# The second FFN projection of a decoder block in seven block products over all 22 k tiles

## The chip, the core and the metric

One Trainium2 chip, one of its cores. The kernel is one launch on that core; the metric is the device time of one execution in microseconds. The program's work is spread over the core's engines, which run side by side and each take their own instructions in order: TensorE (PE; its weight loads are listed apart as PEld), VectorE (DVE), ScalarE (ACT), GpSimd (POOL) and SyncE (SP). SP issues most of the DMAs, POOL and ACT some.

## The reference

One decoder block for 512 tokens of width 1024, in float32: a conditioned RMSNorm, one wide input projection, a gated MLP mixer beside sparse attention, an output projection with a gated residual, and then the FFN. What matters here is the end of it:

```python
x = x + gate1 * (merged @ w_out)
h2 = rms_norm(x, norm2_g) * (1.0 + scale2) + shift2
f_g, f_u = jnp.split(h2 @ w_ffn_in, 2, axis=-1)        # 1024 -> 2 x 2816
x = x + gate2 * ((jax.nn.silu(f_g) * f_u) @ w_ffn_out) # 2816 -> 1024
return rms_norm(x, final_norm_g)
```

The second FFN projection multiplies the gated activations, 512 tokens by 2816, with `w_ffn_out`, 2816 by 1024. 2816 is 22 k tiles of 128.

## The kernel before

**Precision.** TensorE multiplies rounded float32 (fp32r). Every operand is therefore split in a high part (ACT copies it to fp32r) and a low part (DVE subtracts the high part from the source), and a product is three matmuls: high by high, high by low, low by high (`mm3`, lines 53 to 55).

**The stream of weights.** `stream` is a list, in order of use, of weight chunks of 512 KB (128 partitions by two k tiles by 512 columns in the last stage). `issue` starts a chunk's DMA on SP into one of three `raw` buffers, `prep` makes its high part on ACT (line 112) and its low part on DVE (line 116) into one of three `hi` and three `lo` buffers, and `get(i)` prepares up to the second chunk after `i`. So ACT's copy for a chunk waits until TensorE has left the chunk three places before it.

**Seven products in place of eight.** Three projections are computed as 2 by 2 block matrices with seven block products and sums of blocks (Winograd's form): the output projection in part (`oprod`), the first FFN projection (the loop over `q` from line 1627), and the second FFN projection (`zprod`, line 1736). In the second FFN projection, a block is 256 tokens by ten k tiles and ten k tiles by 512 columns: 20 of the 22 k tiles (`KZ`). The two other k tiles (`KC`, 20 and 21) are multiplied in the ordinary way, between the fifth and the sixth product: `W_FO`, lines 1807 to 1813, 48 matmuls of 512 columns. The products come in the order A11, S1, S2, A12, S3, A22, S4. Each is five chunks; for each chunk there are two token tiles of 128, with six matmuls each. Results lie in the eight PSUM banks, and are copied or added between banks where a product contributes to several output blocks (`z_copy`, `z_out`, `z_add`).

**The activations' blocks and their sums.** `a_hi`, `a_lo` and `a_sum` make the high part, the low part and the difference for part `c` of a block, three parts to a block (four, four and two k tiles). They are listed by hand as tasks beside the chunks of each `zprod`: a chunk's tasks are issued after `get` for that chunk and ahead of its matmuls.

**The weights' sums.** The sums of weight blocks are made in DRAM by DMAs that POOL issues, and that copy or accumulate (`wsum_steps`, lines 292 to 314): five groups, one for each chunk position, of six steps; steps 0 and 1 have two DMAs each, the others one. Step 1 accumulates onto what step 0 wrote, step 2 copies what step 1 made, step 3 accumulates onto that, and so on. One call of `wstep` (line 318) issues the next step: ACT writes one element (line 323), POOL copies it (line 324, which ties POOL to ACT's place in the program), and POOL issues the DMAs (lines 305 and 307). After every three steps one call is empty. The loop over `q` has 20 rounds with two calls each, and these 40 calls use up the list of 30 steps and 10 empty places.

**The output projection.** Lines 1418 to 1470 finish it: for each half of the tokens and each half of the columns, two chunks of weights, so eight blocks of twelve matmuls. Between them DVE adds the residual (`resid`), ACT makes the sums of squares, and `row_rstd` (line 1237) gives each token tile its scale: DVE reduces, and POOL raises to the power -1/2 (line 1239). `row_rstd` for tiles 0 and 1 comes after the fourth block, for tiles 2 and 3 after the eighth. `norm2_x` scales the tokens with it (on DVE for even tiles, line 1253, on ACT for odd ones, line 1251), and `norm2_T` transposes them on TensorE (line 1273) and hands them to ACT (lines 1278 and 1281) and DVE (line 1282). Tiles 0 and 1 are transposed within the last block, tiles 2 and 3 within the first groups of the FFN, which otherwise follow at once (line 1599).

**The end.** During A22 and S4, `res_` adds the residual of an output tile that is final (lines 1229 and 1230 on DVE, 1231 on ACT) and multiplies it with the final gain (line 1715 on DVE). `done` finishes a token tile. The last chunks of S4 run token tile by token tile: tile 0 in matmuls of 512 columns, tile 1 in matmuls of 256.

Of the kernel before, what the change touches and what calls it, by code (L numbers as in the profile page):

```python
# [28 lines left out]
def block_kernel(ctx: ExitStack, tc: tile.TileContext, x, positions, w_ada, b_ada, w_in,  # L29
# [239 lines left out]
    KZ = ([0, 1, 2, 3, 4, 5, 6, 7, 12, 13], [8, 9, 10, 11, 16, 17, 18, 19, 14, 15])  # L269
    KC = [20, 21]  # L270
    NZ = 5

    dram = ctx.enter_context(tc.tile_pool(name="dram", bufs=1, space=bass.MemoryType.DRAM))
    wsum = {n: dram.tile([NZ * 256, 512], F32, name=f"wsum{n}") for n in (1, 2, 3, 4)}
    W_Z = {}

    def add_z(key):
        W_Z[key] = []
        for c in range(NZ):
            if key in wsum:  # L280
                src, k0, c0 = wsum[key], 2 * c, 0
            else:
                src, k0, c0 = w_ffn_out, KZ[key[0]][2 * c], key[1] * 512
            W_Z[key].append(add_w(src, [k0, k0 + 1], c0, 512))

    for key in ((0, 0), 1, 2, (1, 0), 3):
        add_z(key)
    W_FO = [add_w(w_ffn_out, KC, 512 * h, 512) for h in range(2)]
    for key in (4, (1, 1)):
        add_z(key)  # L290

    def wsum_steps():

        def step(c, *moves):
            o = slice(256 * c, 256 * c + 256)

            def fn():
                for n, add, src in moves:
                    if isinstance(src, tuple):
                        k = KZ[src[0]][2 * c] * 128  # L300
                        src = w_ffn_out[k:k + 256, 512 * src[1]:512 * src[1] + 512]
# [16 lines left out]
    def wstep():  # L318

        fn = wsteps.pop(0) if wsteps else None  # L320
        if fn:
            t = sm[:, 20 + len(wsteps):21 + len(wsteps)]
# [1095 lines left out]
    for half in range(2):  # L1418
        for h in range(2):
# [124 lines left out]
    za = {}  # L1544
# [7 lines left out]
    def a_part(name, c):  # L1552
        kh, th = AT_[name]
        t = gz[((0, 1, 3), (2, 4, 3))[kh][c]]
        if c == 2:
            t = t[:, 2 * kh:2 * kh + 2]
        return t[:, :, th * 256:(th + 1) * 256]

    def a_hi(key, c):
        h = ZA[key][c]  # L1560
        if c == 2:
# [164 lines left out]
    def zmm(o, ka, c, e, w, cc, start, stop):  # L1726
        ah, al = za[ka, c // 2]
        wh, wl = w
        for j in range(2):
            k_ = 2 * (c % 2) + j  # L1730
            a = tuple(t[:, k_, e * 128:(e + 1) * 128] for t in (ah, al))
            mm3(o, a, (wh[:, j, cc], wl[:, j, cc]), start and j == 0, stop and j == 1, skip_group_check=True)
# [41 lines left out]
    fng, gs = [], []  # L1774
# [5 lines left out]
    def g_hi():  # L1780
        t = ffn[0].tile([128, 2, 2, S], F32R, name="gs", tag="E0", bufs=1)
        gs.extend((t[:, 0], t[:, 1]))
        A.activation(gs[0], gz[5], AF.Copy)

    def g_lo():
        V.tensor_sub(gs[1], gz[5], f(gs[0]))

    zprod(0, "A11", (0, 0), True, [[outs_left, hi_("S1", 0)], [lo_("S1", 0), hi_("S1", 1)],
                                   [lo_("S1", 1), hi_("S1", 2), sm_("S2", 1), lo_("S1", 2)],
                                   [sm_("S2", 2), hi_("S2", 0)], [lo_("S2", 0), hi_("S2", 1)]])  # L1790
    z_copy(1, 0, -1.0)
    zprod(3, "S1", 1, True, [[lo_("S2", 1), hi_("S2", 2), sm_("S4", 0), lo_("S2", 2)], [sm_("S4", 1), hi_("A12", 0)],
                             [sm_("S4", 2), lo_("A12", 0)], [hi_("A12", 1)],
                             [lo_("A12", 1), hi_("A12", 2)]])
    z_out(3)
    zprod(1, "S2", 2, False, [[lo_("A12", 2), sm_("S3", 0)], [sm_("S3", 1)], [sm_("S3", 2), hi_("S3", 0)],
                              [lo_("S3", 0), hi_("S3", 1)], [lo_("S3", 1), hi_("S3", 2)]])
    z_copy(2, 1, -1.0)
    zprod(0, "A12", (1, 0), False, [[lo_("S3", 2), hi_("A22", 0)], [lo_("A22", 0), lambda: z_add(1, 3, V.tensor_add)],
                                    [hi_("A22", 1)], [lo_("A22", 1), hi_("A22", 2)], [lo_("A22", 2)]])  # L1800
    zprod(2, "S3", 3, False, [[hi_("S4", 0)], [lo_("S4", 0), hi_("S4", 1)], [lo_("S4", 1), hi_("S4", 2)],
# [109 lines left out]
```

## Time and profile before

| | |
|---|---|
| median of three runs | 824.95 us (824.74 to 825.56) |
| the profiled execution | 825.28 us |
| its span, first to last instruction | 823.4 us |
| TensorE busy | 808.5 us, 98% of the span |
| VectorE busy | 684.9 us, 83% |
| ScalarE, GpSimd busy | 427.7 us and 156.5 us |
| output projection's last eight blocks | from about 455.6 us |
| first FFN projection | from 479.7 us |
| second FFN projection | from 705.9 us, last matmul at 815.7 us |

The views of the profile used below are the page's summary, the busy times by stretches of time, the waits of an engine, and the timeline of an engine. A timeline's row gives start and length in microseconds, the engine, the source line, the operation, what it writes and reads, and in brackets how long the engine stood idle before it and what ended that. A matmul's length is modelled; since matmuls overlap, what one costs is the distance between the starts.

### The profile page before, as it was taken

The numbers are of one execution on the slowest core, as the hardware profiler recorded it, in microseconds if no ns is written. First come the engines' busy times: TensorE is split into PE (matmuls) and PEld (weight loads), VectorE is DVE, ScalarE is ACT, GpSimd is POOL, SyncE is SP. The second block draws the span as 40 slices with busy tenths as digits, with TensorE's granted clock in tenths as the row PEclk, the third lists the DMA queues.
The fourth block names the chain that finished last, engine by engine and source line by source line (L and its number), as shares of the span: only waits on it lengthen the run. The fifth ranks groups of instructions, "written<-read, shape, count | busy, mean of one in ns | idle before, by whom it ended". The sixth has DMA issues, their size and how long they took to land.

```text
span 823.4 us, 12920 instructions
## 1 busy us (share of the span) xinstructions
PE 808.5 (98%) x4920; PEld 722.0 (88%) x4920; DVE 684.9 (83%) x1167; ACT 427.7 (52%) x760; POOL 156.5 (19%) x171
## 2 busy tenths in 40 slices
PE   7999999999999999999999999999999999999996
PEld 6889889988888888988888899999999999888785
DVE  7989788798899558887688879889989888798676
ACT  6674444323332226665636586555555556666543
POOL 3060031362354411000000010222212222000001
PEclk9999999999999999999999999999999999999998
DMA  9974352332346553046630504889988978766543
GB/s 293 311 211 119 103 179 78 107 100 91 112 136 199 185 174 102 26 153 209 198 132 12 194 27 138 200 263 244 288 221 237 213 220 185 226 203 205 180 128 128
DMA packets 107197, 138.46 MB, mean 168 GB/s; under 512 B 6480, under 2 KB 77136, under 8 KB 106976
## 3 DMA queue, kind: packets, MB, share of 16 engines
q1 hardware_dynamic: 96832, 109.76, 42.8%
q0 software_dynamic: 9584, 27.07, 14.1%
q8 instruction: 38, 0.62, 0.3%
q10 hardware_dynamic: 720, 0.82, 0.3%
q14 instruction: 23, 0.19, 0.1%
HBM read 135.26 MB, written 23.07 MB: 192 GB/s over the span
## 4 chain that ended last, share of the span: by engine, by line
PE 51%; DVE 19%; DMA 5%; ACT 2%; issue 2%; POOL 0%; POOLq 0%; ACTq 0%; DVEq 0%
PE R L53 6%; PE R L54 6%; PE R L55 6%; DMA mraw<-in_w_ada_dram 5%; PE pfo L55 3%; PE pfo L54 3%; PE pfo L53 3%; DVE acc L177 3%; DVE sco L717 2%; DVE m L713 2%; PE pb L53 2%; PE pb L55 2%; PE pb L54 2%; DVE lo L116 2%; PE po L54 2%
## 5 line engine op out<-in xcount | busy, mean ns | idle before, releaser
L112 ACT ACTIVATE hi<-raw 128x1024 fp32r<-128x1024 f32 (+2 forms) x103 | 107.0, 1040 | 106.0 <-PE pb L54 35.7
L116 DVE TENSOR_TENSOR lo<-raw,hi 128x1024 fp32r<-128x1024 f32 (+2 forms) x67 | 81.1, 1214 | 29.4 <-ACT hi L112 28.9
L116 POOL TENSOR_TENSOR lo<-raw,hi 128x1024 fp32r<-128x1024 f32 x29 | 73.0, 2521 | 128.1 <-ACT hi L112 122.4
L53 PE MATMUL pb<-h,hi 128*128 128x512 f32 (+1 forms) x192 | 74.6, 388 | 0.0
L55 PE MATMUL pb<-h,lo 128*128 128x512 f32 (+1 forms) x192 | 73.9, 385 | 0.0
L54 PE MATMUL pb<-h,hi 128*128 128x512 f32 (+1 forms) x192 | 73.9, 385 | 0.0
L54 PE MATMUL pfo<-lo,za 128*128 128x512 f32 (+1 forms) x146 | 56.4, 386 | 0.3 <-DVE lo L116 0.3
L55 PE MATMUL pfo<-hi,za 128*128 128x512 f32 (+1 forms) x146 | 56.2, 385 | 0.0
L53 PE MATMUL pfo<-hi,za 128*128 128x512 f32 (+1 forms) x146 | 56.2, 385 | 0.0
L177 DVE SCALAR_TENSOR_TENSOR acc<-mraw,cols,acc 128x512 f32<-128x512 f32 x49 | 39.8, 813 | 19.6 <-DMA mraw<-in_w_ada_dram 18.6
L1239 POOL TENSOR_TENSOR sm<-sm,mhalf 128x1 f32<-128x1 f32 x8 | 5.3, 660 | 216.9 <-DVE sm L1238 216.9
L53 PE MATMUL R<-tb,sx 128*128 128x256 f32 x160 | 45.3, 283 | 1.1 <-ACT R L1661 0.7
L54 PE MATMUL R<-tb,sx 128*128 128x256 f32 x160 | 45.1, 282 | 0.0
L55 PE MATMUL R<-tb,sx 128*128 128x256 f32 x160 | 45.0, 281 | 0.0
L55 PE MATMUL R<-tb,lo 128*128 128x256 f32 x160 | 44.8, 280 | 0.0
L53 PE MATMUL R<-tb,hi 128*128 128x256 f32 x160 | 44.8, 280 | 0.0
L54 PE MATMUL R<-tb,hi 128*128 128x256 f32 x160 | 44.6, 279 | 0.0
L55 PEld LDWEIGHTS pb<-h,lo 128*128 128x128 f32 x192 | 36.0, 188 | 7.3
L54 PEld LDWEIGHTS pb<-h,hi 128*128 128x128 f32 x192 | 36.0, 188 | 6.9
L53 PEld LDWEIGHTS pb<-h,hi 128*128 128x128 f32 x192 | 36.0, 188 | 6.9
L324 POOL COPY sm<-sm 128x1 f32<-128x1 f32 x30 | 18.9, 631 | 117.0 <-ACT sm L323 116.9
L54 PE MATMUL pav<-lo,h 128*128 128x256 f32 x128 | 35.8, 279 | 0.0
(377 smaller groups left out, 2675.4 us busy)
## 6 DMA issues: line engine op xcount, KB each, us to landing
raw<-in_w_ffn_in_dram SPq DMA_DIRECT2D x44, 512.0 KB, 5.8
raw<-in_w_in_dram SPq DMA_DIRECT2D x40, 512.0 KB, 3.8
wsum<-in_w_ffn_out_dram POOLq DMA_DIRECT2D x30, 512.0 KB, 7.0
mraw<-in_w_ada_dram SPq DMA_DIRECT2D x28, 512.0 KB, 4.1
raw<-wsum SPq DMA_DIRECT2D x20, 512.0 KB, 3.9
raw<-in_w_ffn_out_dram SPq DMA_DIRECT2D x18, 512.0 KB, 4.5
s<-in_w_ada_dram SPq DMA_DIRECT2D x30, 256.0 KB, 5.6
wsum<-wsum POOLq DMA_DIRECT2D x10, 512.0 KB, 5.9
```

The source lines that it names most:

```text
L53: T.matmul(o, wh, rh, start=start, stop=False, **kw)
L54: T.matmul(o, wh, rlo, start=False, stop=False, **kw)
L55: T.matmul(o, wlo, rh, start=False, stop=stop, **kw)
L112: A.activation(hi[:, :m], e["raw"][:, :m], AF.Copy)
L116: e["lo"].tensor_sub(lo[:, :m], e["raw"][:, :m], f(hi[:, :m]))
L177: V.scalar_tensor_tensor(o, w, cs[:, j:j + 1], o, op0=OP.mult, op1=OP.add)
L324: P.tensor_copy(t, t)
L713: V.max(m8s[i], sco[i])
L717: V.match_replace(out=sco[i], in_to_replace=m8s[i], in_values=sco[i], imm_value=TAKEN)
L1239: P.tensor_tensor(r2[:, tk:tk + 1], r2[:, tk:tk + 1], mhalf[:, :1], op=OP.pow)
```

## The change

All 22 k tiles go through the seven products. A half block is eleven k tiles (`KZ`), and a product has six chunks, the last of one k tile and half the size. The separate 48 matmuls, their two chunks (`W_FO`), and the activations' split for them (`g_hi`, `g_lo`) are gone. Each block's activations get a fourth part of one k tile, whose high and low parts lie in a tile of their own (`zl`, in the place `S2_3` where the final gain was; the final gain moves to `E0`, and its load from the end of S3 to its beginning). The lists of tasks are written anew: `res_` for six output tiles, four of them in A22 and two in S4, becomes three and three. The end keeps two and a half chunks of S4 in place of three for the work by token tile, and so three chunks of S4 run before it in place of two.

The weights' sums become six groups of six steps, the last group at half the size, with 12 empty places: 48 calls. The eight calls that this is more are in the output projection's last eight blocks, one after each block's matmuls, so that the sums begin there. The column of the element that `wstep` writes is counted anew.

```diff
-    KZ = ([0, 1, 2, 3, 4, 5, 6, 7, 12, 13], [8, 9, 10, 11, 16, 17, 18, 19, 14, 15])
-    KC = [20, 21]
-    NZ = 5
+    KZ = ([0, 1, 2, 3, 4, 5, 6, 7, 12, 13, 20], [8, 9, 10, 11, 16, 17, 18, 19, 14, 15, 21])
+    NZ = 6
...
-    wsum = {n: dram.tile([NZ * 256, 512], F32, name=f"wsum{n}") for n in (1, 2, 3, 4)}
+    wsum = {n: dram.tile([11 * 128, 512], F32, name=f"wsum{n}") for n in (1, 2, 3, 4)}
...
-            W_Z[key].append(add_w(src, [k0, k0 + 1], c0, 512))
-
-    for key in ((0, 0), 1, 2, (1, 0), 3):
+            W_Z[key].append(add_w(src, [k0, k0 + 1][:1 + (c < 5)], c0, 512))
+
+    for key in ((0, 0), 1, 2, (1, 0), 3, 4, (1, 1)):
         add_z(key)
-    W_FO = [add_w(w_ffn_out, KC, 512 * h, 512) for h in range(2)]
-    for key in (4, (1, 1)):
-        add_z(key)
...
         def step(c, *moves):
-            o = slice(256 * c, 256 * c + 256)
+            n_ = 256 if c < 5 else 128
+            o = slice(256 * c, 256 * c + n_)
...
-            t = sm[:, 20 + len(wsteps):21 + len(wsteps)]
+            k = 20 + sum(w is not None for w in wsteps)
+            t = sm[:, k:k + 1]
...
                     opt_a_mm(po[e], 2 * half + e, hi, lo, stream[i]["kts"], mT, 8, False)
+                wstep()
                 if (half, h, n_) == (0, 0, 0):
                     ensure(WF0[1])
                     s_issue(-2)
...
-        ah, al = za[ka, c // 2]
+        ah, al = za[ka, c // 2 if c < 5 else 3]
         wh, wl = w
-        for j in range(2):
-            k_ = 2 * (c % 2) + j
+        for j in range(1 + (c < 5)):
+            k_ = 2 * (c % 2) + j if c < 5 else 0
...
-        fng.append(base.tile([128, D], F32, name="fng", tag="S2_3", bufs=1))
+        fng.append(ffn[0].tile([128, D], F32, name="fng", tag="E0", bufs=1))
...
-    zprod(2, "S3", 3, False, [[hi_("S4", 0)], [lo_("S4", 0), hi_("S4", 1)], [lo_("S4", 1), hi_("S4", 2)],
-                              [lo_("S4", 2), g_hi], [g_lo, load_fng]])
+    zprod(2, "S3", 3, False, [[hi_("S3", 3), load_fng], [lo_("S3", 3), hi_("S4", 0)], [lo_("S4", 0), hi_("S4", 1)],
+                              [lo_("S4", 1), hi_("S4", 2)], [lo_("S4", 2), hi_("A22", 3)], [lo_("A22", 3)]])
     z_out(2)
     z_add(3, 2, V.tensor_sub)
-
-    for h in range(2):
-        hi, lo = get(W_FO[h])
-        for tk in range(4):
-            o = (Z[h] if tk < 2 else Z[2 + h])[tk % 2]
-            for j in range(2):
-                mm3(o, tuple(t[:, j, tk * 128:(tk + 1) * 128] for t in gs), (hi[:, j], lo[:, j]), False, True,
-                    skip_group_check=True)
...
-    zprod(2, "A22", 4, False, [[res_(0, 0)], [sq_, res_(1, 0)], [sq_, res_(2, 1)], [sq_, res_(3, 1)], [sq_]])
+    zprod(2, "A22", 4, False, [[res_(0, 0)], [sq_, res_(1, 0)], [sq_], [res_(2, 1)], [sq_, hi_("S4", 3)], [lo_("S4", 3)]])
...
-    zprod(1, "S4", (1, 1), False, [[res_(2, 0)], [sq_, res_(3, 0)]])
+    zprod(1, "S4", (1, 1), False, [[res_(3, 1)], [sq_, res_(2, 0)], [sq_, res_(3, 0)]])
     last = bank(7, "pfo")
     A.activation(last[:, :256], Z[1][1][:, 256:], AF.Copy)
-    ids = W_Z[1, 1][2:]
+    ids = W_Z[1, 1][3:]
     ch = [get(i, 2 - k) for k, i in enumerate(ids)]
...
-                zmm(o, "S4", 2 + n_, tk, w, c, False, n_ == 2)
+                zmm(o, "S4", 3 + n_, tk, w, c, False, n_ == 2)
```

The lists of the four products A11, S1, S2 and A12 change in the same way: the high and low parts of the fourth part and its sums are put between the old tasks, and one or two old tasks move one chunk later.

More of the change, by code (lines that the diff above doesn't have):

```diff
@@ L1553, in a_part @@
         kh, th = AT_[name]
-        t = gz[((0, 1, 3), (2, 4, 3))[kh][c]]
-        if c == 2:
-            t = t[:, 2 * kh:2 * kh + 2]
+        t = gz[((0, 1, 3, 5), (2, 4, 3, 5))[kh][c]]
+        if c >= 2:
+            n = 4 - c
+            t = t[:, n * kh:n * kh + n]
         return t[:, :, th * 256:(th + 1) * 256]
     def a_hi(key, c):
-        h = ZA[key][c]
-        if c == 2:
+        h = (ZA[key] + (None,))[c]
+        if c == 3:
+            if not zl:
+                zl.append(base.tile([128, 2, 2, 1, 256], F32R, name="zl", tag="S2_3", bufs=1))
+            t = zl[0][:, ("A11", "S1", "S2", "A12", "S3", "A22", "S4").index(key) % 2]
+            t = (t[:, 0], t[:, 1])
+        elif c == 2:
             t = (base if h[0] == "S" else ffn[0]).tile([128, 2, 2, 256], F32R, name="za", tag=h, bufs=1)
```

36 lines of the change are left out of this document (16 added, 20 removed).

## The prediction

> **What bounds the kernel now.** I read the page's summary first, then the busy times by stretches, then TensorE's waits, and last the timelines of single engines around the two places that the diff touches.
>
> ```profile
> span 823.4 us, 12920 instructions
> PE 808.5 (98%) x4920; PEld 722.0 (88%) x4920; DVE 684.9 (83%) x1167; ACT 427.7 (52%) x760; POOL 156.5 (19%) x171
> ...
> 456.00:469.00 13.00, 13.00 (x58) 10.55 (x58) 11.70 (x15) 6.20 (x11) 0.00 (x0) 1.00 0.73 236
> 469.00:486.00 17.00, 17.00 (x110) 15.33 (x109) 14.12 (x24) 13.37 (x26) 2.23 (x4) 1.00 0.00 0
> ...
> 720.00:745.00 25.00, 25.00 (x110) 20.26 (x109) 24.05 (x25) 15.74 (x19) 0.00 (x0) 1.00 0.64 199
> ...
> 806.90:815.90 9.00, 8.68 (x54) 7.35 (x52) 7.42 (x16) 4.05 (x9) 1.67 (x3) 1.00 0.31 117
> 815.90:823.40 7.50, 0.03 (x1) 0.00 (x0) 2.53 (x7) 2.10 (x6) 0.66 (x1) 0.69 0.37 140
> ...
> PE pfo L54 <- DVE lo L116: 0.3, 1, 0.3
> PE pfo L55 <- DVE gs L1786: 0.3, 1, 0.3
> ```
>
> A row of stretches gives its length, then the busy time of PE, PEld, DVE, ACT and POOL, the granted clock, the DMA engines' share and GB/s. TensorE is busy 98% of the span and in the second FFN projection waits twice for 0.3 us. So a matmul less is worth its issue time, as long as nothing else takes over. The candidates show in the same rows: DVE is busy 24.05 of 25 us in the first products, and the last 7.5 us are a tail without TensorE.
>
> **TensorE's saving.**
>
> ```profile
> 787.34 0.40 PE L53 MATMUL pfo<-hi,za 128*128 128x512 f32 x1
> ...
> 790.14 0.40 PE L53 MATMUL pfo<-hi,za 128*128 128x512 f32 x1
> ...
> 487.88 0.28 PE L53 MATMUL pf<-h,wx 128*128 128x256 f32 x1
> 488.00 0.28 PE L54 MATMUL pf<-h,wx 128*128 128x256 f32 x1
> ...
> 488.24 0.93 PE L1273 MATMUL x2T<-cst,xn 128*128 128x128 f32 x7
> ```
>
> The first two rows are one chunk apart: twelve matmuls in 2.80 us, 0.233 us each; at 256 columns it is 0.12 us. Before, the projection has 7 x 60 + 48 = 468 matmuls in the 512-column unit, 18 of them run as 36 of 256. After it has 7 x 66 = 462, 15 of them run as 30. That saves 3 x 0.233 + 6 x 0.12 = 1.4 us. No more than that can come from TensorE. The low-part wait on `gs` (0.3 us) goes too.
>
> **The front of the projection.** In A11 and S1, DVE gets four low parts and sums of 256 columns in A11, one in S1 (0.45 us or less each, the step from 816.21 to 816.66 in the rows further down), and a half chunk's low part (0.6) in each. That is some 15 us of DVE work per product of 15.4 us of TensorE. Laid out in the order of the tasks, the low part for S1's first chunk ends 0.4 us late; the last sums of the loop are half as large, so their DMAs lighten the chunk loads that DVE starts from. I take 0 to 0.4, 0.2. After S3 the cover of the 48 matmuls is gone: A22 writes the bank that `z_out` copies. ACT's copy of 0.6 us (774.40, first row of the next fence) now stands behind the preparation of a chunk (1.06) within a half chunk's 1.4 us: X + 0.2 + 1.06 + 0.6 against X + 1.4, so 0.45 us of wait. `z_add` delays DVE there by 1.4 us, which its later pauses take up. The five DMAs more (42 chunk loads for 37, 0.75 MB) go down SP between others with three buffers and cost nothing while a load of 4 us has three chunk times. The final gain's load moves on POOL past nothing, since POOL is idle there, and lands some 12 us ahead of use.
>
> **The end of the projection.**
>
> ```profile
> 774.40 0.60 ACT L1755 ACTIVATE ps<-pfo 128x512 f32<-128x512 f32 x1 [0.34 <-PE pfo L55]
> ...
> 787.54 1.06 ACT L112 ACTIVATE hi<-raw 128x1024 fp32r<-128x1024 f32 x1 [4.54 <-PE pfo L55]
> ...
> 788.63 1.23 DVE L116 TENSOR_TENSOR lo<-raw,hi 128x1024 fp32r<-128x1024 f32 x1 [4.37 <-ACT hi L112]
> 789.78 0.68 DVE L1229 TENSOR_TENSOR rt<-pfo,gate2b 128x512 f32<-128x512 f32 x1
> ...
> 791.83 1.22 DVE L116 TENSOR_TENSOR lo<-raw,hi 128x1024 fp32r<-128x1024 f32 x1
> ...
> 801.11 0.39 PE L53 MATMUL pfo<-hi,za 128*128 128x512 f32 x1
> ...
> 810.09 0.15 DVE L1238 TENSOR_REDUCE sm<-ss 128x1 f32<-128x5 f32 x1
> ...
> 812.68 0.69 DVE L1229 TENSOR_TENSOR rt<-pfo,gate2b 128x512 f32<-128x512 f32 x1
> ...
> 816.21 0.42 DVE L1229 TENSOR_TENSOR rt<-pfo,gate2b 128x256 f32<-128x256 f32 x1
> 816.66 0.42 DVE L1230 TENSOR_TENSOR xr<-xr,rt 128x256 f32<-128x256 f32 x1
> ...
> 815.65 0.28 PE L55 MATMUL pfo<-hi,za 128*128 128x256 f32 x1
> ```
>
> These rows give DVE's prices: a chunk's low part 1.15 us, a residual with its gain 2.05 (789.78 to 791.83), finishing two tiles 2.59 (810.09 to 812.68), and from there 3.53 to the last residual at 816.21. Eight low parts, six residuals and the finishing sum to 8 x 1.15 + 6 x 2.05 + 2.59 = 24.1 us, which is the whole distance from 788.63 to 812.68: DVE makes no pause. TensorE's last matmul ends at 815.65 + 0.28 = 815.93. Both arrive together.
>
> Let U be S4's start, 801.1 before. On the way to U TensorE has 36 matmuls more (six in the sixth chunk of each of the six products ahead) and 48 fewer: it is there 12 x 0.233 = 2.8 us earlier. After U, DVE now has more: it may start S4's second low part only after ACT's copy, which waits for the start of A22's half chunk at U - 1.4 (as 787.54 and 788.63 stand to TensorE's 787.34: 0.2 + 1.06 + 0.03 later), so at U - 0.1. Then: low parts 4 x 1.15, one of 0.6 and one of 0.34, three residuals 6.15, finishing 2.59, which sums to 14.3: tile 0's residual starts at U + 14.2 where it started at U + 11.6 (812.68) before. The last residual comes at U + 17.7 against U + 15.1, 2.6 us later; TensorE itself is done at U + 8.4 + 15 x 0.233 + 30 x 0.12 = U + 15.5. So what TensorE gains ahead of U, DVE loses behind it: -2.8 + 2.6 = -0.2. With 0.2 + 0.45 of new waits and 0.3 gone, the whole projection comes to +0.15 us. Ends: -1.7 if DVE keeps up (1.4 + 0.3), +0.5 with all waits.
>
> **The sums in the output projection.** This is where I expect the change to cost.
>
> ```profile
> 454.67 1.06 ACT L112 ACTIVATE wx<-raw 128x1024 fp32r<-128x1024 f32 x1 [2.54 <-DMA raw<-in_w_out_dram]
> 470.68 1.16 ACT L1251 ACTIVATE xn<-xr,sm 128x1024 f32<-128x1024 f32 x1 [0.42 <-POOL sm L1239]
> 486.73 1.15 ACT L1251 ACTIVATE xn<-xr,sm 128x1024 f32<-128x1024 f32 x1 [1.29 <-POOL sm L1239]
> ...
> 469.24 1.40 POOL L1239 TENSOR_TENSOR sm<-sm,mhalf 128x1 f32<-128x1 f32 x2 [92.30 <-DVE sm L1238]
> 484.84 0.55 POOL L1239 TENSOR_TENSOR sm<-sm,mhalf 128x1 f32<-128x1 f32 x1 [14.19 <-DVE sm L1238]
> ...
> 482.67 0.69 DVE L1282 TENSOR_TENSOR h<-h2f,h 128x512 fp32r<-128x512 f32 x1 [0.36 <-ACT h L1281]
> ...
> 555.55 0.91 POOL L305 DMA_DIRECT2D wsum<-in_w_ffn_out_dram  x1
> ...
> 564.23 0.52 POOL L307 DMA_DIRECT2D wsum<-wsum  x1 [4.55 <-DMA wsum<-in_w_ffn_out_dram]
> 529.73 0.89 POOL L305 DMA_DIRECT2D wsum<-in_w_ffn_out_dram  x1
> 535.95 0.52 POOL L307 DMA_DIRECT2D wsum<-wsum  x1 [0.55 <-DMA wsum<-in_w_ffn_out_dram]
> 543.11 0.87 POOL L305 DMA_DIRECT2D wsum<-in_w_ffn_out_dram  x1 [3.35 <-DMA wsum<-wsum]
> ...
> DMA to landing us min/median/max: 3.8/6.0/7.0
> ...
> DMA to landing us min/median/max: 5.9/8.2/13.8
> ...
> 459.60 0.37 SPq L92 DMA_DIRECT2D raw<-in_w_ffn_in_dram  x1
> 460.14 1.47 SPq L1302 DMA_DIRECT2D raw<-in_w_ffn_in_dram  x3
> ```
>
> Before, POOL is free when the power -1/2 is wanted (469.24, 484.84). The transposes of tiles 2 and 3 start on TensorE at 488.24, and the scaled tile 3 is ready at 486.73 + 1.15 = 487.88: 0.4 us of slack. A delay of `row_rstd` beyond that is TensorE's.
>
> The idle time of 4.55 us at 564.23 shows how POOL takes these steps: its queue stands until the DMA before has landed, and what is behind waits as well. Behind it now stand both pairs of powers: tiles 0 and 1 behind steps 0 to 2, tiles 2 and 3 behind all six. The two landing rows are copies (line 307) and accumulations (line 305), both from the loop, where the DMA engines are loaded.
>
> Step 0 can go once ACT has done its copy of 454.67: 455.7, plus 0.4 for ACT's element and POOL's copy, 456.1. Landing at the median of copies, 6.0, with 0.3 to issue: step 1 at 462.4. Its accumulation meets the four loads of 459.60 to 461.6. The nearest rows are the group at 555.55, made among the loop's loads: step 2 followed 8.7 us later, at 564.23. That puts step 2 at 471.1 and POOL free at 471.6, 2.4 us after 469.24. DVE, ACT and the residuals of the second half follow one another from there, with pauses like the 0.36 before 482.67 as the only slack, so TensorE loses about 2.2 us, first at the FFN's start and then at the transposes. From 469 the DMA engines stood idle (share 0.00 in the second row of stretches), so the other steps take prices near the shortest: copy 5.0 (it still meets the second accumulation), accumulation 6.2 (529.73 to 535.95), copy 4.1, with issue: step 5 leaves POOL at 487.6, as late as the delayed residuals want it. Both ways give 2.2.
>
> Lower end: shortest prices throughout (3.8 and 5.9, 0.3 to issue) put step 2 at 466.4; step 3 has to wait for ACT's place behind the scaling at 470.68, about 474, and step 5 leaves POOL at about 485: no stall. Upper end: the pace of the loop (6.0, 8.7, 6, 6.2, and 7.2 from 535.95 to 543.11, with issues) puts step 5 off POOL at 491.7; two powers (1.4) and ACT's scaling (1.15) later tile 3 is ready at 494.3, 5.9 us after TensorE wants it. I take 2.2, since one half of the chain runs among loads and the other alone.
>
> The Trainium skill, "DMA: Bandwidth & Descriptors", section "Anatomy of one DMA — SWDGE (gpsimd) path", gives a DMA from GpSimd as 2.0 us plus its bytes at 436 GB/s, which for 512 KB is an estimate of 3.2 us. By that the six steps are through by 475 and the sum of this part is 0. The trace's shortest is 3.8 and its accumulations 5.9, so I do not go by it.
>
> Small parts: ACT's six elements (about 0.1 each) and POOL's copies lie beside. The gate load behind step 5 on POOL is needed a hundred microseconds later. The loop's 40 calls do the same steps one group on, the last group with half the bytes.
>
> **Sum.** 825.28 (the profiled execution, 823.4 span and 1.9 around it) + 0.15 + 2.2 = 827.6. That execution is 0.33 above the median of 824.95, so 827.3 for the median.
>
> **Rivals.**
>
> - *The sums are through in time*, and DVE's end takes the saving: 824.95 + 0.15 = 825.1. For it: the idle DMA engines from 469 on and the shortest landings. Against: four loads beside step 1. The page of the skill named above speaks for this one.
> - *The saving arrives, faster*: the sums are in time and DVE's work after U is not what ends last: 824.95 - 1.4 - 0.3 = 823.2. It decides from the point where tile 0's last residual starts by U + 12.3, as TensorE has it ready; by DVE's prices it starts 1.9 us later. For it: DVE has about 2.7 us of pauses in A22 that another order would fill.
> - *The sums at the loop's pace*: 5.9 us of stall, 824.95 + 0.15 + 5.9 = 831.0. For it: all landing rows are from the loop. Against: a DMA share of 0.00. The granted clock of 0.69 in the row where TensorE stands idle shows that a long pause could also cost speed. The skill's "TensorE: Matmul & The Clock Gate", section "What's actually happening", has the clock halve after an idle window of about 3.4 us; by that a single stall of this length would cost up to some 1.7 us more. No stall of that length inside the work is in this trace.
>
> **How the numbers follow.** Forecast 0.44 (825.9 to 828.6), first rival 0.20 (824.3 to 825.9), second 0.18 (822.3 to 823.9), third 0.15 (828.6 to 832), anything else 0.03. Within 0.2%, about what a measurement of this kernel can tell from no change, is 823.3 to 826.6: it holds the first rival, a quarter of the forecast (0.10) and 0.04 of the second, so 0.34. Faster keeps 0.14, slower 0.34 + 0.15 + 0.03 = 0.52. The range leaves out about a tenth on each side: 822.8 to 830.8.
>
> **What would show it.** Right: in the output projection POOL's powers start behind a wsum DMA, later than the reduce that feeds them; TensorE waits some 2 us between 479 and 491; the distance from A11's first matmul to S4's first shrinks by 2.3 to 2.8 us; at the end DVE has no pause from S4's start on, and the last residual starts about 2 us after its matmul. Wrong: TensorE without a pause in the output projection (first rival), or an end in which DVE waits for TensorE (second), or waits in A11 and S1 of more than half a microsecond.

## The result, and the profile after

The changed kernel takes 829.25 us (median of 6 runs, 828.58 to 830.16). The kernel before took 825.0 us beside it (6 runs, 824.74 to 826.51). The ratio is 1.0052, with a 95% interval of 1.0042 to 1.0061: 4.25 us slower, where 827.3 and a range of 822.8 to 830.8 were predicted. The profiled execution took 829.07 us with a span of 827.3, against 825.28 and 823.4 before.

The page's summary of the changed kernel:

```profile
span 827.3 us, 12970 instructions
...
PE 809.0 (98%) x4911; PEld 722.4 (87%) x4911; DVE 689.5 (83%) x1182; ACT 432.0 (52%) x777; POOL 165.8 (20%) x185
```

TensorE's instructions are nine fewer in the records, and it is busy as long as before (809.0 against 808.5 us). The summary doesn't say where the time went; the stages do. TensorE's timeline of the changed kernel has the first matmul of each stage and the last one of all (start, length, engine, line, operation, what is written and read):

```profile
455.68 0.39 PE L53 MATMUL po<-wx,mt 128*128 128x512 f32 x1
...
482.39 0.39 PE L53 MATMUL pf<-h,wx 128*128 128x256 f32 x1 [1.56 <-ACT h L1279]
...
509.13 0.28 PE L53 MATMUL R<-h,sa 128*128 128x256 f32 x1
...
709.96 0.40 PE L53 MATMUL pfo<-hi,za 128*128 128x512 f32 x1
...
817.82 0.28 PE L55 MATMUL pfo<-hi,zl 128*128 128x256 f32 x1
```

The differences of these starts, and those of the same matmuls before, give a table of the stages in us:

| stage | before | after | difference |
|---|---|---|---|
| output projection's last eight blocks | 23.84 | 26.71 | +2.87 |
| first FFN projection, ahead of the loop | 24.53 | 26.74 | +2.21 |
| the loop over `q` | 201.68 | 200.83 | -0.85 |
| second FFN projection, to the start of its last matmul | 109.77 | 107.86 | -1.91 |
| from there to the end of the span | 7.76 | 9.47 | +1.71 |

With the stretch ahead of these (-0.14) they make up the 3.9 us between the two spans. The two last rows almost cancel, as predicted. The loss is in the first two, 5.1 us where 2.2 stood in the prediction, and the loop gives 0.85 back.

In the two stages that lose, POOL's timeline of the changed kernel shows the order of things:

```profile
455.64 1.15 POOL L322 COPY sm<-sm 128x1 f32<-128x1 f32 x1 [78.83 <-ACT sm L321]
456.74 1.17 POOL L304 DMA_DIRECT2D wsum<-in_w_ffn_out_dram  x2
...
463.39 0.98 POOL L302 DMA_DIRECT2D wsum<-in_w_ffn_out_dram  x1 [2.49 <-DMA wsum<-in_w_ffn_out_dram]
464.54 0.88 POOL L302 DMA_DIRECT2D wsum<-in_w_ffn_out_dram  x1 [0.17 <-issue]
...
473.01 0.53 POOL L304 DMA_DIRECT2D wsum<-wsum  x1 [4.63 <-DMA wsum<-in_w_ffn_out_dram]
473.56 1.41 POOL L1237 TENSOR_TENSOR sm<-sm,mhalf 128x1 f32<-128x1 f32 x2
...
488.30 0.90 POOL L302 DMA_DIRECT2D wsum<-in_w_ffn_out_dram  x1 [3.46 <-DMA wsum<-wsum]
489.26 0.57 POOL L1237 TENSOR_TENSOR sm<-sm,mhalf 128x1 f32<-128x1 f32 x1
```

These are the copy that ties POOL to ACT's place, step 0, step 1 with its two DMAs, step 2, the powers of tiles 0 and 1, step 5, and the first power of tiles 2 and 3. POOL stands still for 4.63 us at step 2, waiting for what step 1 accumulates, and the powers come right behind. What the powers need from DVE was there four microseconds earlier, and DVE then waits for them, in its own timeline of the changed kernel:

```profile
469.31 0.22 DVE L1236 TENSOR_REDUCE sm<-ss 128x1 f32<-128x5 f32 x2
474.18 0.75 DVE L1251 TENSOR_SCALAR xn<-xr,sm 128x1024 f32<-128x1024 f32 x1 [4.66 <-POOL sm L1237]
```

Counted from the stage's first matmul, the powers start at 473.56 - 455.68 = 17.88 us, where they started at 469.24 - 455.82 = 13.42 before: 4.46 us of delay. TensorE's waits in the changed kernel show where it arrives:

```profile
PE pf L53 <- ACT h L1279: 1.6, 1, 1.6
PE x2T L1271 <- ACT xn L1249: 0.9, 1, 0.9
...
PE pf L54 <- DVE h L1280: 0.3, 1, 0.3
...
PE pfo L53 <- ACT ps L1760: 0.3, 1, 0.3
```

The first three are the transposes of the first tiles and the FFN's first matmuls, 2.8 us in all. A further 1.4 us of the 5.1 is 15 matmuls of the FFN that ran 0.213 us apart in place of 0.12 (15 x 0.093). The last 0.9 us I did not trace matmul by matmul; the first starts behind a pause lie further apart than later ones. At the transposes of tiles 2 and 3 TensorE doesn't wait. The stretches of the changed kernel (length; busy time of PE, PEld, DVE, ACT, POOL; granted clock; DMA share; GB/s) show the reason for the 15:

```profile
475.00:483.20 8.20, 5.43 (x31) 4.18 (x30) 6.92 (x10) 7.28 (x15) 2.28 (x3) 1.00 0.40 72
483.20:487.10 3.90, 3.90 (x21) 3.90 (x22) 3.50 (x6) 3.81 (x9) 0.74 (x2) 0.56 0.38 134
```

After the pauses the granted clock is 0.56 on average over 3.9 us, "the half clock" below. What that costs is a question for the experiments.

At the end, DVE's timeline of the changed kernel has tile 0's last residual and the very last one, and TensorE's has S4's first matmul:

```profile
802.06 0.39 PE L53 MATMUL pfo<-hi,za 128*128 128x512 f32 x1
...
816.27 0.68 DVE L1227 TENSOR_TENSOR rt<-pfo,gate2b 128x512 f32<-128x512 f32 x1
...
819.80 0.42 DVE L1227 TENSOR_TENSOR rt<-pfo,gate2b 128x256 f32<-128x256 f32 x1
```

With U = 802.06 these are U + 14.21 and U + 17.74; U + 14.2 and U + 17.7 were predicted. Between U and the first of them DVE pauses only twice, 0.7 us each, for POOL's powers of the finished tiles, as it did before.

### The profile page after: what moved, and what is told of

Its sections match the earlier page's. It is cut to its first block, busy times and chain, and to the rows that moved or that the text cites. A ratio compares the mean times of both kernels' runs of the same rounds, so it can differ in the third digit from the quotient of the medians.

```text
span 827.3 us, 12970 instructions
## 1 busy us (share of the span) xinstructions
PE 809.0 (98%) x4911; PEld 722.4 (87%) x4911; DVE 689.5 (83%) x1182; ACT 432.0 (52%) x777; POOL 165.8 (20%) x185
## 4 chain that ended last, share of the span: by engine, by line
PE 87%; DVE 3%; DMA 3%; ACT 2%; issue 2%; POOL 1%; SPq 0%; POOLq 0%; DVEq 0%; ACTq 0%
PE pb L55 9%; PE pb L53 9%; PE pb L54 9%; PE R L53 8%; PE R L54 8%; PE R L55 8%; PE pfo L53 4%; PE pfo L55 4%; PE pfo L54 4%; PE pav L54 2%; PE pav L53 2%; PE pav L55 2%; PE pgb L53 2%; PE pgb L54 2%; PE pgb L55 2%
## 5 line engine op out<-in xcount | busy, mean ns | idle before, releaser
L112 ACT ACTIVATE hi<-raw 128x1024 fp32r<-128x1024 f32 (+2 forms) x108 | 109.4, 1014 | 105.4 <-PE pfo L55 29.5
L116 DVE TENSOR_TENSOR lo<-raw,hi 128x1024 fp32r<-128x1024 f32 (+2 forms) x72 | 83.5, 1163 | 24.4 <-ACT hi L112 24.1
L322 POOL COPY sm<-sm 128x1 f32<-128x1 f32 x36 | 23.5, 652 | 199.0 <-ACT sm L321 199.0
L53 PE MATMUL pav<-hi,h 128*128 128x256 f32 x128 | 35.7, 279 | 0.0
```

The lines of the kernel that those rows point to most:

```text
L53: T.matmul(o, wh, rh, start=start, stop=False, **kw)
L112: A.activation(hi[:, :m], e["raw"][:, :m], AF.Copy)
L116: e["lo"].tensor_sub(lo[:, :m], e["raw"][:, :m], f(hi[:, :m]))
L322: P.tensor_copy(t, t)
```

## The experiments

Each ran four to eleven times, beside the kernel before on the same chip; `e9_behind` and `e10_before_two` were on another chip than the rest. The two middle columns give, from each profile, the first two rows of the table above together and the loop; the last gives the second projection with what follows.

| run | median us | ratio to before, 95% interval | two stages | loop | second projection to the end |
|---|---|---|---|---|---|
| before | | | 48.37 | 201.68 | 117.53 |
| changed kernel | 829.25 | 1.0052, 1.0042 to 1.0061 | 53.45 | 200.83 | 117.33 |
| e1_loop | 828.82 | 1.0044, 1.0028 to 1.0061 | 48.38 | 203.16 | 121.91 |
| e2_before_early | 829.61 | 1.0051, 1.0036 to 1.0065 | 53.11 | 200.59 | 117.40 |
| e3_two | 824.52 | 0.9993, 0.9984 to 1.0001 | 48.73 | 200.68 | 117.33 |
| e4_fill | 829.29 | 1.0049, 1.0035 to 1.0063 | 53.45 | 200.70 | 117.33 |
| e5_tail | 823.36 | 0.9981, 0.9971 to 0.9990 | 48.92 | 200.68 | 115.85 |
| e6_three | 829.17 | 1.0055, 1.0035 to 1.0076 | 52.89 | 200.93 | 117.33 |
| e7_second | 830.46 | 1.0068, 1.0047 to 1.0089 | 54.13 | 200.67 | 117.34 |
| e8_fill_less | 828.88 | 1.0048, 1.0032 to 1.0065 | 53.55 | 202.43 | 117.34 |
| e9_behind | 825.35 | 1.0002, 0.9991 to 1.0012 | 48.79 | 200.68 | 117.33 |
| e10_before_two | 824.70 | 0.9990, 0.9980 to 0.9999 | 48.89 | 200.51 | 117.40 |

My theory: the loss is POOL's order, that is, powers standing behind a DMA that waits; the seven products over 22 k tiles change nothing to speak of. Rivals: the DMAs themselves slow the loads around them; the half clock makes the loss; the products or the loop have a part in it.

### One part alone: the early sums on the kernel before

```diff
+                wstep()
                 if (half, h, n_) == (0, 0, 0):
...
-        return [fn for k in range(0, len(order), 3) for fn in order[k:k + 3] + [None]]
+        return [fn for k in range(0, len(order), 3) for fn in order[k:k + 3] + [None]] + [None] * 8
```

> The kernel before, with the second part of the change alone: the first eight calls of its 48 in the output projection, the FFN projection as it was. If the loss is the place of the sums, it shows here without the new blocks: 825.0 + 5.1 = 830.1 less at most 0.9 for a wait in the loop that may shift, so 829.2 to 830.1. If the new blocks are needed for the loss, 825 or below.

The column of `wstep`'s element is counted anew as in the changed kernel. Without any of the new products it takes 829.61 us: the whole loss. TensorE's longest waits in this stage are 1.6 and 0.9 us, at the same two places as in the changed kernel. The early sums alone do it.

### The other part alone: no early sums

In `e1_loop` the changed kernel has no call in the output projection, and the loop's 40 calls hold 36 steps and 4 empty places.

```diff
-                wstep()
                 if (half, h, n_) == (0, 0, 0):
...
-        return [fn for k in range(0, len(order), 3) for fn in order[k:k + 3] + [None]]
+        return [fn for k in range(0, len(order), 9) for fn in order[k:k + 9] + [None]]
```

> The changed projection with no sums in the output projection: 36 steps and 4 empty places in the loop's 40 calls. If the whole loss of the changed kernel lies in the output projection (waits of TensorE and the half clock after them, 5.1 us between its start and the loop in the profile), this runs at 829.25 - 5.1 = 824.2, and TensorE has no pause between 455 and 500. If a part of the loss is in the second FFN projection itself, it stays above 825. A rival: the denser loop pays, POOL falls behind and the last sums are late for A22 or S4, with waits of raw loads on wsum after 770.

The two stages are back at 48.38 us, but the time is lost elsewhere: in the profiled execution, the longest of 8 (831.76 us; the shortest is 826.29), 1.5 us in the loop and 4.4 in the second projection with the end. Its waits on TensorE, and the last step in POOL's timeline:

```profile
PE pfo L54 <- DVE lo L116: 2.8, 6, 0.9
...
PE R L53 <- ACT ps L1685: 1.1, 1, 1.1
PE R L53 <- ACT R L1665: 0.9, 1, 0.9
```

```profile
723.58 0.80 POOL L302 DMA_DIRECT2D wsum<-in_w_ffn_out_dram  x1 [3.86 <-DMA wsum<-wsum]
```

In the changed kernel the last step left POOL ahead of the second projection:

```profile
705.79 0.80 POOL L302 DMA_DIRECT2D wsum<-in_w_ffn_out_dram  x1 [0.26 <-issue]
```

Here it leaves 18 us later, and TensorE waits six times for low parts of chunks, 2.8 us in all, five of them between 715 and 737 us. The expectation had such waits after 770. So this list, which starts with the loop and has nine steps to ten calls, doesn't fit; with a head start of two steps it does (`e3_two`). Whether the waits come from the late sums themselves or from their DMAs beside the chunks' loads, this run doesn't separate.

### Two early steps only

```diff
-                wstep()
+                if (half, h) == (0, 0):
+                    wstep()
...
-        return [fn for k in range(0, len(order), 3) for fn in order[k:k + 3] + [None]]
+        return order[:2] + [fn for k in range(2, len(order), 6) for fn in order[k:k + 6] + [None]]
```

> The changed kernel with steps 0 and 1 alone in the output projection, at the same two places, and the other 34 in the loop. The same four DMAs meet the same loads, but nothing that waits stands ahead of the four powers on POOL. If POOL's order is the cause: TensorE's waits between 474 and 490 are gone but for 0.4 us, no half clock, 824.2 to 825. If the DMAs' contention with the loads is the cause (they land up to 5 us later), the scaling still comes late: 828 or more.

824.52 us. Steps 0 and 1 run as in the changed kernel, and no powers stand behind a DMA that waits for them, in POOL's timeline of this run:

```profile
465.10 0.88 POOL L302 DMA_DIRECT2D wsum<-in_w_ffn_out_dram  x1 [0.29 <-DMA wsum<-in_w_ffn_out_dram]
470.20 1.41 POOL L1237 TENSOR_TENSOR sm<-sm,mhalf 128x1 f32<-128x1 f32 x2 [4.21 <-DVE sm L1236]
```

It is DVE that the powers wait for now. The accumulations of step 1 are the same here, so they are not what costs. Steps 2 to 5 are gone, and with them both the waiting and the load of their DMAs; `e9_behind` below tells these apart.

### Which pair of powers costs

`e6_three` keeps three early steps, so the first pair of powers stands behind step 2 and the second behind nothing. `e7_second` frees the first pair and puts steps 2 to 5 ahead of the second.

```diff
 e6_three
+        return order[:3] + [None] * 5 + [fn for k in range(3, len(order), 5) for fn in order[k:k + 5] + [None]]
 e7_second
+        rest = [fn for k in range(6, len(order), 3) for fn in order[k:k + 3] + [None]]
+        return order[:2] + [None] * 2 + order[2:6] + rest
```

> The changed kernel with only steps 0, 1 and 2 in the output projection and the other 33 in the loop. So POOL's powers for tiles 0 and 1 stand behind step 2 as in the changed kernel, and those for tiles 2 and 3 behind nothing. Theory A (the delay of the first powers runs on through VectorE and ScalarE to the transposes of the second tiles): the first powers again near 473.6, TensorE's pauses of about 0.9 and 1.6 us ahead of the FFN's first groups stay, and the time stays near 829 us. Theory B (the second pair behind step 5 is what costs): first powers late, but the second pair near 485 to 487, one pause of a us or so, and about 825 to 826 us.

> The changed kernel with steps 0 and 1 in the first two blocks of the output projection, two empty calls, then steps 2 to 5 in the last four blocks; the loop does the rest. The powers for tiles 0 and 1 stand behind step 1 only (free, near 470), those for tiles 2 and 3 behind step 5. Theory A (the first pair decides): the second pair's powers come when step 5 has left POOL, near 489, so the last tile is scaled about 492.3 where it was wanted near 488.5: a pause of up to 3 us at one place only, some 827.5 us; less if step 2, which no longer stands in front of the powers, starts earlier. Theory B (the second pair is the cost): the whole loss of the changed kernel comes back, 829 us.

POOL's timelines, of `e6_three`:

```profile
473.19 0.53 POOL L304 DMA_DIRECT2D wsum<-wsum  x1 [4.54 <-DMA wsum<-in_w_ffn_out_dram]
473.73 1.41 POOL L1237 TENSOR_TENSOR sm<-sm,mhalf 128x1 f32<-128x1 f32 x2
489.34 0.55 POOL L1237 TENSOR_TENSOR sm<-sm,mhalf 128x1 f32<-128x1 f32 x1 [14.20 <-DVE sm L1236]
```

and of `e7_second`:

```profile
469.36 1.41 POOL L1238 TENSOR_TENSOR sm<-sm,mhalf 128x1 f32<-128x1 f32 x2 [4.21 <-DVE sm L1237]
...
488.71 0.88 POOL L302 DMA_DIRECT2D wsum<-in_w_ffn_out_dram  x1 [3.42 <-DMA wsum<-wsum]
489.30 1.71 POOL L1238 TENSOR_TENSOR sm<-sm,mhalf 128x1 f32<-128x1 f32 x2
```

`e6_three` went as theory A says: 829.17 us. One waiting DMA, 4.54 us of idle POOL, holds the first pair back, and the second pair then waits for DVE, which is late itself. Counted as above, the first pair is late by 473.73 - 455.62 - 13.42 = 4.69 us and the two stages by 4.52: the delay goes through TensorE almost undiminished.

`e7_second` came out above both expectations, 830.46 us where 827.5 or 829 was expected, with 829 at the edge of its interval. The first pair is on time, but the second starts 489.30 - 455.58 = 33.72 us into the stage, where it started at 484.84 - 455.82 = 29.02 before: 4.7 us late, as late as in the changed kernel (489.26 - 455.68 = 33.58). Step 5 left POOL about when I had expected it. What I had left out of the pause of up to 3 us is what follows it: TensorE waits 2.7 us, then 0.8 more, and over the 5.3 us from the end of the first wait its granted clock is 0.70. Each pair is enough to lose the time. The two losses do not add: in the changed kernel the first delay moves the second pair to where step 5 leaves POOL anyway, 488.30 against 489.26.

### The same DMAs behind the powers

```diff
-                wstep()
+                if half + h == 0 or (half, h, n_) == (1, 0, 0):
+                    wstep()
...
                 norm2_x(0)
+                wstep()
...
                 norm2_x(1)
+                wstep()
+                wstep()
...
+        return order[:6] + [fn for k in range(6, len(order), 3) for fn in order[k:k + 3] + [None]]
```

> The changed kernel with all six early steps kept in the output projection, but with none of them ahead of a power that it could hold up: steps 0 and 1 in the first two blocks, step 2 behind the powers and scaling of tiles 0 and 1, step 3 in the fifth block, steps 4 and 5 behind those of tiles 2 and 3. The same DMAs run in about the same time, so that their load on the DMA engines stays and only their place in POOL's queue changes. If the place is the cause: powers near 470 and 486 again, the two stages at 48.5 to 49 us in place of 53.5, and 824.5 us in all. If the DMAs beside the FFN's first groups slow the loads there: powers early, but TensorE waits for operands made from late chunks, and 826 us or more.

POOL's timeline of this run:

```profile
470.79 1.41 POOL L1237 TENSOR_TENSOR sm<-sm,mhalf 128x1 f32<-128x1 f32 x2 [4.09 <-DVE sm L1236]
...
474.01 0.58 POOL L304 DMA_DIRECT2D wsum<-wsum  x1 [0.29 <-issue]
...
478.85 0.92 POOL L302 DMA_DIRECT2D wsum<-in_w_ffn_out_dram  x1 [3.93 <-DMA wsum<-wsum]
486.39 0.57 POOL L1237 TENSOR_TENSOR sm<-sm,mhalf 128x1 f32<-128x1 f32 x1 [6.62 <-DVE sm L1236]
```

All six early steps are there. Step 3 waits on POOL for 3.93 us, where in the changed kernel it was step 2 that waited, and nothing that is wanted stands behind it. Steps 4 and 5 are issued some six microseconds later than in the changed kernel. The two stages take 48.79 us in place of 53.45. So the place in POOL's queue is the cause, and the DMAs themselves cost no more than the 0.4 us that the two stages take longer than before; `e3_two` and `e10_before_two` show 0.4 and 0.5 with steps 0 and 1 alone. In time it is 825.35 us, 0.85 above the 824.5 expected. Its interval and that of `e3_two` overlap. Its profile has no stage for the difference: the stages sum to within 0.1 us of those of `e3_two`, and the stretch ahead of them is 0.5 us longer.

### The pauses filled

In `e4_fill` (8 and 14) and `e8_fill_less` (4 and 7) TensorE multiplies the identity with itself, a result that nobody reads, ahead of the first transposes and of the FFN's first matmuls:

```diff
+            for _ in range(8 if half + k2 == 0 else 0):
+                T.matmul(p[:, :128], ident, ident, start=True, stop=True)
...
+    for _ in range(14):
+        T.matmul(pf[0][0][:, :128], ident, ident, start=True, stop=True)
```

> The changed kernel with 22 matmuls of 128 columns that nobody reads, put where TensorE waits: 8 ahead of the first transposes and 14 ahead of the first matmuls of the FFN, about 0.11 us each, so they lie in the waits of 0.9 and 1.6 us. If the stretch of 3.9 us at a granted clock of 0.56 comes from the pauses, it goes, and the time falls by about 1.6 us to 827.6. If that stretch has another cause, or pauses this short do not matter for the clock, 829.3 as it was.

> The changed kernel with 4 and 7 filler matmuls, whose results nobody reads, ahead of the first transposes and of the FFN's first matmuls. At the 0.217 us that one took in the run with 8 and 14, they fill 0.9 and 1.5 us, about what TensorE otherwise stands still there. If the half clock after those pauses costs time: no row of the granted clock at half near 483 to 487, and up to 0.8 us faster than the changed kernel, 828.5 us. If the next wait (the second tiles' scale near 491) sets the end of the stage, the clock makes no difference and it is 829.3 us again.

829.29 and 828.88 us; neither differs from the changed kernel by more than the intervals leave open. The granted clock stayed at 1.00 in both, as their stretches from 475 to 490 us show, and yet the two stages take 53.45 and 53.55 us, as long as with the half clock. Neither run is clean, though. A filler took 0.217 us, twice what I had reckoned, so the 14 of `e4_fill` overshot their wait by about 1.4 us. The four of `e8_fill_less` stand ahead of the transposes, while the wait lies between the first tile's and the second's; it stayed, with 0.8 us. Above all, step 2 waited longer in both than in the changed kernel (5.30 and 5.23 us for 4.63), so the powers came later. POOL's timeline of `e4_fill`, step 2 and the second pair:

```profile
475.32 0.53 POOL L304 DMA_DIRECT2D wsum<-wsum  x1 [5.30 <-DMA wsum<-in_w_ffn_out_dram]
...
491.56 0.68 POOL L1237 TENSOR_TENSOR sm<-sm,mhalf 128x1 f32<-128x1 f32 x1
```

What the half clock costs shows when the two stages are divided at the start of the second pair of powers (in us, from POOL's and TensorE's timelines):

| run | stages' start to second powers | second powers to the loop | lowest granted clock behind the pauses |
|---|---|---|---|
| before | 29.02 | 19.35 | 1.00 |
| changed kernel | 33.58 | 19.87 | 0.56 over 3.9 us |
| e2_before_early | 34.01 | 19.10 | 1.00 |
| e6_three | 33.72 | 19.17 | 1.00 |
| e4_fill | 34.29 | 19.15 | 1.00 |
| e8_fill_less | 34.39 | 19.17 | 1.00 |
| e7_second | 33.72 | 20.41 | 0.70 over 5.3 us |
| e3_two | 29.54 | 19.18 | 1.00 |
| e9_behind | 29.63 | 19.17 | 1.00 |

Wherever the sums start early and the clock is full, the loop starts 19.10 to 19.18 us after the second powers, however late these are. The changed kernel needs 0.7 us more than that, and `e7_second` 1.2. So the half clock costs the changed kernel some 0.7 us in its profiled execution, half of its 1.4: in `e2_before_early` two waits of 0.2 and 0.4 us for operands stand where the slow matmuls were. Against the kernel before, its 5.1 us are 4.6 of later powers (33.58 - 29.02) and 0.5 behind them. These are single profiles; the medians are too close together to show 0.7 us.

### The loop

```diff
-        return [fn for k in range(0, len(order), 3) for fn in order[k:k + 3] + [None]]
+        return order[:2] + [fn for k in range(2, len(order), 3) for fn in order[k:k + 3] + [None]] + [None] * 2
...
+                if (half, h) == (0, 0):
+                    wstep()
```

> The kernel before with steps 0 and 1 of its sums in the output projection and 28 in the loop. The loop of the kernel before has a pause of 0.9 us near 616 that was gone in the changed kernel and in the runs whose loop begins the list further on. If beginning the list earlier is what takes it away: the loop at 200.6 to 200.8 us where it was 201.7, 0.8 us less in all, 824.3 us, and the second projection and the end as before; then the seven products over 22 k tiles, with the same head start, bring about 0.2 us more only. If the pause has another cause: 825.2 us as before.

824.70 us, 0.1% faster than before, at the edge of what its interval tells, and the loop at 200.51 us in its profile. The pause near 616 us (0.74 us of idle, 0.9 from start to start) is gone from the kernel before as well with a head start of two steps; so the loop's 0.85 us goes with the sums' timing and not with the products. It isn't settled what in that timing decides: `e8_fill_less` has the changed kernel's list, step for step, and a loop of 202.43 us with pauses of up to 0.9.

This run and `e3_two` differ only in the second projection, its sums and their pace in the loop. In the last column `e3_two` is 0.07 us shorter, and by its ratio 0.03% longer: with this order of tasks, the seven products over 22 k tiles make no difference that these runs can tell.

### One residual moved from S4 to A22

```diff
-    zprod(2, "A22", 4, False, [[res_(0, 0)], [sq_, res_(1, 0)], [sq_], [res_(2, 1)], [sq_, hi_("S4", 3)], [lo_("S4", 3)]])
+    zprod(2, "A22", 4, False, [[res_(0, 0)], [sq_, res_(1, 0)], [sq_], [res_(2, 1)], [sq_, hi_("S4", 3), res_(3, 1)],
+                              [lo_("S4", 3)]])
...
-    zprod(1, "S4", (1, 1), False, [[res_(3, 1)], [sq_, res_(2, 0)], [sq_, res_(3, 0)]])
+    zprod(1, "S4", (1, 1), False, [[sq_, res_(2, 0)], [sq_, res_(3, 0)], [sq_]])
```

> The kernel with two early steps (824.52 us in its run) with one residual task moved: that of tile 3's second half goes from S4's first chunk to the fifth chunk of A22, and the two others go one chunk earlier in S4. If VectorE sets the end, because three residuals lie behind the start of S4 (tile 0's residual began 14.2 us after it): one residual of about 2 us less behind it, tile 0's residual near 12.8 us after the start of S4, TensorE ready for it at about 12.3, and a total 1 to 1.5 us less: 823.0 to 823.5 us. If the end hangs on TensorE or on the last stores: 824.5 us, no change. If the residual in A22 pushes S4's low parts back so that TensorE waits there: up to 1 us slower, 825.5 us.

The edit stands on `e3_two`. DVE's timeline around S4's start, of `e3_two`:

```profile
797.72 1.23 DVE L116 TENSOR_TENSOR lo<-raw,hi 128x1024 fp32r<-128x1024 f32 x1 [1.49 <-ACT hi L112]
...
811.95 0.68 DVE L1227 TENSOR_TENSOR rt<-pfo,gate2b 128x512 f32<-128x512 f32 x1
```

and of `e5_tail`, with S4's first matmul from TensorE's timeline:

```profile
796.19 0.69 DVE L1227 TENSOR_TENSOR rt<-pfo,gate2b 128x512 f32<-128x512 f32 x1
...
797.80 0.39 PE L53 MATMUL pfo<-hi,za 128*128 128x512 f32 x1
...
810.53 0.68 DVE L1227 TENSOR_TENSOR rt<-pfo,gate2b 128x512 f32<-128x512 f32 x1
```

The residual fills DVE's pause of 1.49 us. Tile 0's last residual starts at 810.53 - 797.80 = U + 12.7, and the second projection with its end takes 115.85 us in place of 117.33. The chain of work that ended last, from 795 us on, says the same. By lines it is DVE's in `e3_two`, and mostly TensorE's in `e5_tail`:

```profile
by line: issue 16.4%; DVE lo L116 12.3%; DVE xr L1228 8.0%; DVE rt L1227 7.0%; POOL sm L1237 4.8%; DVE xo L1725 3.2%; ACT hi L112 3.1%; ACT rt L1229 2.1%; POOLq L1897 2.0%; PE pfo L55 2.0%; ACT xo L1724 1.8%; PE pfo L53 1.3%; PE pfo L54 1.3
```

```profile
by line: PE pfo L54 11.3%; PE pfo L55 10.6%; PE pfo L53 10.6%; issue 7.8%; DVE lo L116 5.3%; POOL sm L1237 4.8%; DVE xo L1725 3.2%; ACT rt L1229 2.1%; POOLq L1898 2.0%; DVE xr L1228 2.0%; ACT xo L1724 1.8%; DVE rt L1227 1.7%; DVE sm L1236 0
```

At 823.36 us (ratio 0.9981, 0.9971 to 0.9990) this version is faster than both kernels: DVE's order at the end was what kept the saving of the products back. The 1.8 us against the kernel before hold the head start's part as well; beside `e10_before_two`, which has that alone, the intervals overlap, and the stages show 1.55 us less in the second projection with the end. The same move without the new products was not tried.

## Where the prediction was right, and where its size was off

- *The forecast's mechanism was right*: powers behind waiting DMAs on POOL cost the time, and DVE's end takes back what TensorE saves. The size was off: 4.25 us slower where 2.3 was forecast. The time lies in the range, but 0.65 us above the forecast's own bounds (825.9 to 828.6) and in those of the third rival. That the total is off by only 2 us is in part luck: the stall was 2.9 us longer than predicted, and the loop (0.85) and the second projection (0.35) took 1.2 of that back unforeseen.
- *The mis-sized term is the stall in the output projection*, 2.2 us predicted and 5.1 measured, within its ends of 0 and 5.9. Step 0 went at 456.74 (predicted 456.1), step 1 at 463.39 (462.4), step 2 at 473.01 (471.1). The first miss, 0.6 us, is POOL's copy of one element: it took 1.15 us where 0.4 was taken for it and ACT's element together (0.19 for the latter in the kernel before, not the 0.1 that the prediction's small parts have). Step 0's landing adds 0.4. The largest, 0.9 us, is step 1's accumulation, 9.6 us to the next issue where the row from the loop gave 8.7. So POOL's delay was 4.5 us and not 2.4, and no slack of 0.2 was left to take off it. The half clock, 0.7 us, was in no term of the forecast's sum. Both halves of the chain had given the same 2.2; the first, among loads, is enough to lose the time alone, as `e6_three` shows. TensorE waited at the first tiles' transposes and at the FFN's start, and not at the second tiles' transposes, where the prediction had a part of it.
- The Trainium skill, "DMA: Bandwidth & Descriptors", section "Anatomy of one DMA — SWDGE (gpsimd) path", gave an estimate of 3.2 us for such a DMA. It does not hold for these; from 455 to 492 us the changed kernel has medians of 6.6 and 4.2 us from issue to landing:

```profile
wsum<-in_w_ffn_out_dram POOLq DMA_DIRECT2D x6, 512.0 KB, 6.6
wsum<-wsum POOLq DMA_DIRECT2D x2, 512.0 KB, 4.2
```

- *First rival (the sums are through in time)*: false for this order of calls. Its time comes back as soon as the powers stand ahead of the waiting step: `e3_two` and `e9_behind` lie within 0.1% of the kernel before.
- *Second rival (the saving arrives)*: false as the tasks are listed, since tile 0's residual starts at U + 14.2, after the deciding point U + 12.3. `e5_tail` brings it to U + 12.7, 0.4 behind that point, and the second projection with the end is 1.7 us shorter than before, the size of the saving: its reason, DVE's pauses in A22 that another order would fill, was right.
- *Third rival (the loop's pace)*: its reason holds for the first links, which went at the loop's pace and a little slower, and so does its remark that a pause could cost speed (0.7 us). But it put the stall at step 5 ahead of the last powers, and it is made at step 2 ahead of the first.
- *TensorE's saving*: S4's start came 709.96 to 802.06 = 92.10 us after A11's, where it was 705.88 to 801.11 = 95.23: 3.1 us less, where 2.3 to 2.8 was predicted. The rest of 0.3 I did not trace.
- *The front*: the wait of 0 to 0.4 us in A11 and S1 isn't there. The wait at `z_out` is, with 0.3 us where 0.45 was predicted. The whole projection came to -0.2 us in place of +0.15.
- *What the prediction left out*: the loop. It said that the calls do the same steps one group on, and gave no time; the loop was 0.85 us shorter, with the head start.

## What to carry to other kernels

In this kernel a DMA that waited on POOL held up everything behind it on POOL, and two powers of one column inherited its whole wait (4.63 us). Where an engine issues DMAs that wait, issue them behind the computation that others want (`e9_behind`), or stop the chain one step earlier (`e3_two`). Price a chain of dependent DMAs link by link, under the load that each meets: here the first links, beside loads, set the delay. When an engine's work is cut and the end is set by another engine, look for a pause of that other engine ahead of the end, and move a task there (`e5_tail`).

## What the hardware showed that I had not expected

The granted clock fell to 0.56 for 3.9 us after three pauses of TensorE that were each short (0.9, 1.6 and 0.3 us). In `e2_before_early` and `e6_three`, after the same three, it stayed at 1.00. In `e7_second`, around pauses of 2.7 and 0.8 us, it fell to 0.70. The stretch of `e2_before_early`, and the one from the end of the long pause on in `e7_second`:

```profile
483.20:487.10 3.90, 3.53 (x25) 3.13 (x26) 3.66 (x6) 3.80 (x8) 0.71 (x2) 1.00 0.46 143
```

```profile
491.10:496.40 5.30, 4.46 (x25) 4.29 (x26) 2.95 (x4) 5.24 (x9) 0.15 (x1) 0.70 0.80 190
```

The Trainium skill, "TensorE: Matmul & The Clock Gate", section "What's actually happening", names one idle window of about 3.4 us for this. No single pause here was that long. The same pauses gave both outcomes, so something beside their length decides; that stays open.

A filler matmul of 128 fp32 columns took 0.217 us, twice what I had taken from the spacing of the transposes, so 14 of them filled 3.0 us. The trace has two records for each filler (28 for the 14) and one for each transpose.
